# A third head of the down product in the norms' bank, a shorter series, and an earlier place for a layer's small parameters

## The chip, the cores and the metric

The kernel runs on one core of a Trainium2 chip, as one program. The core has a matrix engine (TensorE, in the views PE, with PEld for its weight loads), three engines for elementwise work (VectorE or DVE, ScalarE or ACT, GpSimd or POOL) and SyncE (SP), whose queue issues the DMA transfers here. Each engine works through its own queue of instructions in order; semaphores tie the queues together. The metric is the device time of one execution in microseconds; lower is better. The "span" is the time between the first and the last record of a profiled execution.

## What is computed

Two layers of a hybrid decoder run for one inference step, on a prompt of 512 tokens and on eight sequences of eight tokens that share the weights; all is fp32. Each layer is a feed-forward block, a mixer (sliding-window attention beside a gated linear recurrence) and a second feed-forward block, each ahead of it normed and modulated by vectors from a small conditioning product. Cut to what matters here:

```python
def swiglu(h, w_gate, w_up, w_down):
    return (jax.nn.silu(h @ w_gate) * (h @ w_up)) @ w_down
...
    x = x + FFN_RES * g1 * swiglu(modulate(x, sh1, sc1), w1_gate, w1_up, w1_down)
    h = modulate(x, sh2, sc2)
    z = h @ w_in
...
    xc, new_conv = causal_conv(xr, conv_buf, conv_w, conv_b)
    hs, h_last = rg_lru(xc, h0, w_rg, b_rg, w_ig, b_ig, lru_lambda)
...
    x = x + g2 * (merged @ w_out)
    x = x + FFN_RES * g3 * swiglu(modulate(x, sh3, sc3), w2_gate, w2_up, w2_down)
```

The model is 1024 wide, its hidden layer 2816. In the recurrence, `softplus(-lru_lambda)` is needed for 512 channels and two layers; it depends on parameters alone:

```python
    log_a = -RG_C * r.astype(jnp.float32) * jax.nn.softplus(-lam.astype(jnp.float32))
```

## The kernel before

**Products.** Activations are stored transposed: 128 features a tile, 576 tokens (64 of the eight sequences, then the prompt) in two halves, h=0 and h=1, of 288. An fp32 matrix product is made of three faster ones: each operand is split into a rounded high part, which ScalarE writes (L219), and the low rest, which VectorE or GpSimd subtracts (L220); then high by high, high by low and low by high are summed in one bank of PSUM, the matmul's accumulator memory. So a matmul needs splits of its weights (tiles `wh`, `wl`) and of its activations (tiles in the rings `t`, `u` or `hn`).

**Feed-forward block.** The hidden layer goes by pairs of 128 columns, eleven pairs to a block. A pair loads its gate and up weights (`load_pair`, L617). After the first one or two pairs of a block, which are made plainly, each of the two products of a pair is made by `quad` with seven block products instead of eight. That takes sums of weight blocks, on GpSimd (L849, tiles `P`), and sums of activation blocks, which `sums` prepares once a block on VectorE (L763): for each k of four, a sum `a` in bank tp, from it a sum `b` in bank nrm, from it a sum `c` in bank pv (in the very first block they stand in SBUF instead). The generator is drained by the first pair that wants the sums. In a quad, two of the block results accumulate in banks `pa` and `pe` (both of the name mm), two in banks of the name sc; ScalarE (L870, L882) and VectorE (L858 to L862) combine them, and the product of gate and up is split again into the two hidden halves (L220).

**Groups and heads.** Pairs are gathered into groups of four hidden tiles (two pairs) or of two (one pair): `GROUPS` is (4, 4, 4, 2, 4, 4) for the first block of the first layer and (2, 4, 4, 4, 4, 4) for the other three blocks. Behind a group come its down products: for each of eight output tiles m and each half h the product of the group's hidden tiles with the down weights, and `update` (L593, L595, L598, VectorE) adds the result to the residual stream, which empties the bank. So that TensorE has work while the group's last pair is still being combined, `head()` starts four of these products with the hidden tiles of the earlier pair (`slice(0, nf - 2)`), and `down` ends them later. Where a group has two hidden tiles, that slice is empty, so that the heads there only take their banks. `halves` is true for the last group of a block, and for a first group of width two: there the down products run all m of h=0 first, and then all m of h=1. In the last group of a block which has a norm behind it (three of four), TensorE's order is pinned, and the last quad's last product (`end_pair`) stands ahead of the third head.

**Banks.** There are eight banks of PSUM: three of the name mm, two sc, and one each of tp, pv and nrm. A tile of a name waits until the earlier tile in that bank has been read. The bank nrm serves the norms, the sums `b`, and one product of the first pair.

**Order.** A planner orders each engine's queue when the program is built, by estimated costs and by the order in which the Python code issues the work; pinned instructions keep a given order.

**Parameters of the recurrence.** `params()` fills one tile by a memset (L407) and fourteen small DMAs on SP's queue (L410 to L418), transposes it, and computes the softplus on tiles of 128x8: an exponential on ScalarE (L430, with a load of its function table) and then, on VectorE, a series for the logarithm (L433 to L440), whose result is kept for both layers. `layer_loads` (L946) clears a tile and issues six more DMAs. Both are called by `start`, in the first block of each layer, ahead of the pair of number START (L634); `params()` in the first layer alone.

Of the kernel before, what the change touches and what calls it, by code (L numbers as in the profile page):

```python
# [15 lines left out]
ALU = mybir.AluOpType  # L16
# [14 lines left out]
FT = DFF // P  # L31
GROUPS = ((4, 4, 4, 2, 4, 4), (2, 4, 4, 4, 4, 4))
NA = (1, 4)
START = 8
ADA0 = 3
PLAIN = ((2, 1), (1, 1))
LATE = (0, 0)
# [116 lines left out]
class Net:  # L154
# [249 lines left out]
    def params(self):  # L404
        nc, I = self.nc, self.I
# [20 lines left out]
        def c8(name):  # L426
            return self.const(name, [P, LC, DEPTH])
        y, s, s2, acc, mx = c8("sy"), c8("ss"), c8("ss2"), c8("sacc"), c8("smx")
# [4 lines left out]
        nc.vector.tensor_tensor(s, s, y, ALU.mult)  # L433
        nc.vector.tensor_tensor(s2, s, s, ALU.mult)
        n = 9
        nc.vector.tensor_scalar(acc, s2, 1.0 / (2 * n + 1), 1.0 / (2 * n - 1), ALU.mult, ALU.add)
        for i in range(n - 2, -1, -1):
            nc.vector.tensor_tensor(acc, acc, s2, ALU.mult)
            nc.vector.tensor_scalar(acc, acc, 1.0 / (2 * i + 1), None, ALU.add)
        nc.vector.scalar_tensor_tensor(acc, acc, 2.0, s, ALU.mult, ALU.mult)  # L440
        nc.vector.tensor_scalar(mx, lam, -1.0, 0.0, ALU.mult, ALU.max)
        self.sp2, self.spm4 = c8("sp2"), c8("spm4")
        nc.vector.tensor_tensor(acc, acc, mx, ALU.add)
# [177 lines left out]
    def ffn(self, l, ws, wd, s0, hn, pend, nxt, groups, ada_n, wo=None, open_next=None, start=None, raws=None, after=None):  # L621

        nc, I = self.nc, self.I
# [4 lines left out]
        for gi, nf in enumerate(groups):  # L628
            hid = []
            for fp in range(nf // 2):  # L630
                hts = [(self.slot([P, NT], F32R), self.slot([P, NT], F32R, "u")) for _ in range(2)]
                hid += hts
                pn = f0 // 2 + fp
                if start and pn == START:  # L634
                    start()
# [65 lines left out]
            box, heads = None, []  # L701
            pin = last and nxt is not None
            halves = last or gi == 0 and nf == 2

            def head():

                for n, (m, h) in enumerate(((0, 0), (1, 0), (2, 0), (3, 0)) if halves else ((0, 1), (1, 1), (0, 0), (1, 0))):
                    if n == 2 and (pin or not halves):
                        self.end_pair()
                    heads.append(self.ps(("mm", "sc")[len(heads) % 2]))  # L710
                    self.down_part(heads[-1], h, units[m], hid, nf, slice(0, nf - 2), pin)
                self.end_pair()

# [4 lines left out]
            for c0 in range(0, D, 2 * nw):  # L718
                raw = self.t("raw", [P, 2048]).rearrange("p (k c) -> p k c", k=nf)
                nc.sync.dma_start(raw, I[wd][l].rearrange("(f p) c -> p f c", p=P)[:, f0:f0 + nf, c0:c0 + 2 * nw])  # L720
                for c in range(0, 2 * nw, nw):
                    u = self.wsplit(raw[:, :, c:c + nw], (nf, nw), wo and not gi)
                    units += [(u[0][:, :, j * P:(j + 1) * P], u[1][:, :, j * P:(j + 1) * P]) for j in range(nw // P)]
                    if c0 + c == (HEAD * nw if halves else 0):
                        head()
                        if last:
                            self.hold = self.parts
                    if not halves:
                        for h in (1, 0):
                            for m in range((c0 + c) // P, len(units)):  # L730
                                down(m, h, ("mm", "sc")[m % 2])
# [808 lines left out]
```

## Time and profile before

| | us |
|---|---|
| median of three runs | 2165.23 (2163.7 to 2166.9) |
| the profiled execution | 2164.47 |
| its span | 2162.6 |
| TensorE busy in it | 2091.9 |
| VectorE busy | 1552.9 |
| ScalarE busy | 1022.0 |
| GpSimd busy | 774.9 |

A row of the page's groups, or of the timeline, names an engine, a line of the kernel, an operation, and tiles as out<-in. In the timeline the first number is the start in microseconds and the second the duration; a bracket at the end is the idle time of the engine just before, and what ended it. In the windows, after the stretch's bounds and length, each engine has its busy time and its number of instructions, and behind them stand the granted clock of TensorE (1.00 is full speed), the busy share of the DMA engines and the GB/s. Adjacent matmuls overlap in the records, so that the distance between starts, not the duration, is the price of one.

### The profile page before, as it was taken

The page shows a single profiled execution, that of the slowest core. Times are in us where ns is not written, and L with a number is a line of the kernel's source. Part 1 is how long each engine was busy: PE and PEld are TensorE (multiplying, and loading weights), DVE is VectorE, ACT ScalarE, POOL GpSimd, SP SyncE. Part 2 cuts the span into 40 slices and gives each one's busy share as a digit, 9 for nine tenths or more (in the row PEclk, how much of TensorE's full clock was granted, in tenths as well). Part 3 has the DMA queues.
Part 4 walks back from the last instruction along what each step waited for, and adds up shares of the span by engine and source line. Part 5 has one row for each costly group of instructions (what it writes and reads, how often), then busy time and mean ns, then how long its engine had stood idle before and what let it go on. Part 6 is the DMA issues. An engine that isn't in the chain of part 4 may idle for free.

```text
span 2162.6 us, 40524 instructions
## 1 busy us (share of the span) xinstructions
PE 2091.9 (97%) x15856; PEld 1976.5 (91%) x15856; DVE 1552.9 (72%) x3779; ACT 1022.0 (47%) x2348; POOL 774.9 (36%) x671
## 2 busy tenths in 40 slices
PE   6999999999999999999999999999999999999999
PEld 6889899999878988989999999999997899999998
DVE  5666767675787876576678966776667789677765
ACT  4333435356576433343354543444567664344432
POOL 2242323234426433233245342232552474323430
PEclk8999999999999999999999999999999999999999
DMA  9745633231212165463342323232312022223221
GB/s 306 267 146 182 219 116 130 78 118 46 69 53 80 66 247 195 174 217 137 118 147 69 110 66 98 79 117 79 98 43 79 22 79 79 99 79 117 81 76 45
DMA packets 162365, 250.11 MB, mean 116 GB/s; under 512 B 7276, under 2 KB 125436, under 8 KB 154975
## 3 DMA queue, kind: packets, MB, share of 16 engines
q1 hardware_dynamic: 162018, 247.46, 34.1%
q8 instruction: 124, 2.03, 0.4%
q14 instruction: 67, 0.54, 0.1%
q10 hardware_dynamic: 156, 0.07, 0.0%
HBM read 244.62 MB, written 4.87 MB: 115 GB/s over the span
## 4 chain that ended last, share of the span: by engine, by line
PE 84%; DVE 9%; ACT 3%; DMA 1%; issue 1%; POOL 1%; SPq 0%; ACTq 0%; DVEq 0%; POOLq 0%
PE ps_mm L843 25%; PE ps_mm L206 13%; PE ps_sc L933 11%; PE ps_mm L933 11%; PE ps_sc L843 10%; PE ps_sc L206 7%; DVE wl L220 3%; PE ps_pv L491 2%; PE ps_pv L206 2%; DMA raw<-in_w_ada_dram 1%; PE ps_nrm L206 1%; PE ps_tp L209 1%; ACT wh L219 1%; DVE u L220 1%; ACT t L219 1%
## 5 line engine op out<-in xcount | busy, mean ns | idle before, releaser
L849 POOL TENSOR_TENSOR P<-raw 128x512 f32<-128x512 f32 x156 | 229.2, 1482 | 714.3 <-DVE wl L220 383.1
L219 ACT CAST wh<-raw 128x512 fp32r<-128x512 f32 x498 | 296.7, 620 | 293.8 <-PE ps_sc L933 125.8
L220 DVE TENSOR_TENSOR wl<-raw,wh 128x512 fp32r<-128x512 f32 x408 | 336.5, 839 | 43.6 <-ACT wh L219 28.8
L219 ACT CAST wh<-P 128x512 fp32r<-128x512 f32 x312 | 187.2, 620 | 283.4 <-PE ps_sc L933 193.2
L220 DVE TENSOR_TENSOR wl<-P,wh 128x512 fp32r<-128x512 f32 x312 | 245.4, 803 | 63.4 <-ACT wh L219 56.1
L843 PE MATMUL ps_mm<-hn,wh 128*128 128x288 f32 x1248 | 256.0, 296 | 2.3 <-ACT wh L219 0.8
L843 PE MATMUL ps_sc<-hn,wh 128*128 128x288 f32 x1248 | 255.0, 296 | 0.0
L843 PE MATMUL ps_mm<-t,wh 128*128 128x288 f32 x936 | 221.9, 298 | 2.4 <-DVE ps_mm L861 1.7
L843 PE MATMUL ps_mm<-u,wh 128*128 128x288 f32 x936 | 220.8, 297 | 0.0
L843 PEld LDWEIGHTS ps_mm<-hn,wh 128*128 128x128 f32 x1248 | 199.8, 188 | 14.8 <-ACT t L870 2.9
L843 PEld LDWEIGHTS ps_sc<-hn,wh 128*128 128x128 f32 x1248 | 199.8, 188 | 9.6 <-issue 9.2
L933 PE MATMUL ps_sc<-t,wh 128*128 128x288 f32 x608 | 180.1, 296 | 5.7 <-DVE u L220 4.6
L843 PE MATMUL ps_mm<-u,wl 128*128 128x288 f32 x624 | 184.1, 295 | 0.0
L843 PE MATMUL ps_sc<-hn,wl 128*128 128x288 f32 x624 | 184.1, 295 | 0.0
L843 PE MATMUL ps_mm<-hn,wl 128*128 128x288 f32 x624 | 183.9, 295 | 0.0
L933 PE MATMUL ps_mm<-t,wh 128*128 128x288 f32 x608 | 180.6, 297 | 2.3 <-DVE u L220 1.8
L933 PE MATMUL ps_mm<-t,wl 128*128 128x288 f32 x608 | 179.6, 295 | 1.3 <-DVE wl L220 1.3
L933 PE MATMUL ps_mm<-u,wh 128*128 128x288 f32 x608 | 179.8, 296 | 0.2
L933 PE MATMUL ps_sc<-u,wh 128*128 128x288 f32 x608 | 179.3, 295 | 0.0
L933 PE MATMUL ps_sc<-t,wl 128*128 128x288 f32 x608 | 179.2, 295 | 0.0
L843 PEld LDWEIGHTS ps_mm<-t,wh 128*128 128x128 f32 x936 | 159.1, 189 | 12.1 <-issue 4.6
L849 POOL TENSOR_TENSOR P<-P,raw 128x512 f32<-128x512 f32 x78 | 114.4, 1466 | 154.4 <-DVE wl L220 152.1
(413 smaller groups left out, 5453.2 us busy)
## 6 DMA issues: line engine op xcount, KB each, us to landing
raw<-in_w_ada_dram SPq DMA_DIRECT2D x60, 1024.0 KB
raw<-in_w_gate_dram SPq DMA_DIRECT2D x44, 1024.0 KB
raw<-in_w_up_dram SPq DMA_DIRECT2D x44, 1024.0 KB
raw<-in_w_down_dram SPq DMA_DIRECT2D x44, 1024.0 KB
raw<-in_w_in_dram SPq DMA_DIRECT2D x14, 1024.0 KB
raw<-in_w_ada_dram SPq DMA_DIRECT2D x16, 512.0 KB
raw<-in_w_out_dram SPq DMA_DIRECT2D x4, 1024.0 KB
raw<-in_w_out_dram SPq DMA_DIRECT2D x8, 512.0 KB
```

The lines of the kernel that those rows point to most:

```text
L206: return self.pin(self.nc.tensor.matmul(*a, **k))
L209: return self.pin(self.nc.tensor.transpose(*a, **k))
L219: a = self.nc.scalar.copy(hi, src)
L220: b = (self.nc.gpsimd if pool else self.nc.vector).tensor_tensor(lo, src, hi.bitcast(F32), ALU.subtract)
L491: nc.tensor.matmul(acc[32 * j:32 * j + 32, :n], self.cT[:, k, :], raw[:, j * n:(j + 1) * n], start=(k == 0), stop=(k == KT - 1), tile_posi ...
L843: nc.tensor.matmul(ps[:, :HALF], a[x][:, k, :], b[k][y], start=start and k + n == 0, stop=k == 3 and n == 2, skip_group_check=True)
L849: nc.gpsimd.tensor_tensor(t, s[x] if x == 1 else x, s[y] if y == 2 else y, op)
L933: mm(ps[:, :HALF], u[x][:, f, :], hid[f][y][:, hs], start=f + n == 0, stop=f == nf - 1 and n == 2)
```

## The change

Three things change.

- The third of the four heads takes its bank by the name nrm instead of mm, wherever `halves` is true: in the last group of all four blocks, and in the first group of the three blocks that begin with a group of two.
- The logarithm's series is written with one fused instruction a coefficient, (acc + constant) * s2, in place of a product and an addition: one tensor_scalar, nine scalar_tensor_tensor and one more tensor_scalar for the factor of two, eleven instructions in place of eighteen.
- START goes from 8 to 6: the parameters and the layer's small loads are issued two pairs sooner, in both layers.

```diff
-START = 8
+START = 6
...
-        nc.vector.tensor_scalar(acc, s2, 1.0 / (2 * n + 1), 1.0 / (2 * n - 1), ALU.mult, ALU.add)
-        for i in range(n - 2, -1, -1):
-            nc.vector.tensor_tensor(acc, acc, s2, ALU.mult)
-            nc.vector.tensor_scalar(acc, acc, 1.0 / (2 * i + 1), None, ALU.add)
-        nc.vector.scalar_tensor_tensor(acc, acc, 2.0, s, ALU.mult, ALU.mult)
+        nc.vector.tensor_scalar(acc, s2, 1.0 / (2 * n + 1), None, ALU.mult)
+        for i in range(n - 1, 0, -1):
+            nc.vector.scalar_tensor_tensor(acc, acc, 1.0 / (2 * i + 1), s2, ALU.add, ALU.mult)
+        nc.vector.scalar_tensor_tensor(acc, acc, 1.0, s, ALU.add, ALU.mult)
+        nc.vector.tensor_scalar(acc, acc, 2.0, None, ALU.mult)
...
-                    heads.append(self.ps(("mm", "sc")[len(heads) % 2]))
+                    heads.append(self.ps(("mm", "sc", "nrm" if halves else "mm", "sc")[len(heads)]))
                     self.down_part(heads[-1], h, units[m], hid, nf, slice(0, nf - 2), pin)
```

## The prediction, made before the change was run

> **What bounds the kernel now.** I read the page's first lines, then the chain that ended last, then PE's rows among the waits, and last the stretches around the three places that the diff touches.
>
> ```profile
> span 2162.6 us, 40524 instructions
> PE 2091.9 (97%) x15856; PEld 1976.5 (91%) x15856; DVE 1552.9 (72%) x3779; ACT 1022.0 (47%) x2348; POOL 774.9 (36%) x671
> ...
> PE 84%; DVE 9%; ACT 3%; DMA 1%; issue 1%; POOL 1%; SPq 0%; ACTq 0%; DVEq 0%; POOLq 0%
> ```
> ```profile
> PE ps_mm L206 <- DVE u L220: 6.8, 3, 2.3
> PE ps_sc L933 <- DVE u L220: 4.6, 6, 3.5
> ```
> ```profile
> 270.00:280.00 10.00, 10.00 (x78) 10.00 (x77) 7.20 (x20) 2.29 (x4) 2.31 (x2) 1.00 0.15 50
> 280.00:290.00 10.00, 10.00 (x77) 10.00 (x77) 5.11 (x14) 1.18 (x3) 3.49 (x3) 1.00 0.01 2
> ```
> TensorE bounds it: 97% busy, 84% of the chain. The two waits (total us, times, longest) are nearly all that it loses to DVE's splits on the touched paths. The windows (columns: PE, PEld, DVE, ACT, POOL busy, granted clock, DMA share) give the price of one matmul in a full stretch: 10 us for 77 to 78, 0.13 us. So only a gap on PE, or a slowed PE, counts; everything else is cover. No edit changes the number of matmuls.
>
> **Edit 1, third head in nrm: the last groups.** PE's timeline (start, duration, ..., [idle before, releaser]) and DVE's and ACT's:
>
> ```profile
> 455.19 0.29 PE L843 MATMUL ps_mm<-u,wl 128*128 128x288 f32 x1
> 457.75 0.61 PE L206 MATMUL ps_mm<-t,wh 128*128 128x288 f32 x1 [2.27 <-DVE u L220]
> ...
> 1121.44 0.40 PE L206 MATMUL ps_mm<-t,wh 128*128 128x288 f32 x1 [2.27 <-DVE u L220]
> ...
> 1520.10 0.40 PE L206 MATMUL ps_mm<-t,wh 128*128 128x288 f32 x1 [2.26 <-DVE u L220]
> ```
> ```profile
> 457.24 0.82 DVE L220 TENSOR_TENSOR u<-ps_mm,t 128x288 fp32r<-128x288 f32 x2
> ```
> ```profile
> 452.35 0.40 ACT L882 COPY u<-ps_sc 128x288 f32<-128x288 f32 x1
> ```
> ```profile
> 455.00:461.00 6.00, 3.73 (x18) 3.50 (x17) 3.67 (x8) 2.32 (x5) 1.34 (x1) 0.72 0.06 11
> ```
> At the end of the three feed-forward blocks that have a norm after them, the third head finds all three mm banks held (pa and pe of the last quad, head one) until DVE's splits at 457.24 read them. Its hidden half and weights are ready, and the norms' bank is idle then. So the stalls go: 2.27 + 2.27 + 2.26 = 6.8. The first also trips the clock: 6.00 us at 0.72, 18 matmuls that need 18 x 0.13 = 2.34, so 6.00 - 2.34 - 2.27 = 1.4 lost beside the stall. Sum 8.2. The fourth head's sc bank is free since ACT's copy at 452.35. Late next are the remaining products, whose banks DVE empties; for that I keep back 0.7: **-7.5**. Bounds: -8.2, and -4 if half of each stall comes back one step later. The fourth block has no norm after it; nothing is taken there.
>
> **Edit 1 again: the first groups.** `halves` also holds for a first group of width two, which three of four blocks have. There the heads run no product; they only take banks, so the third one takes nrm for the whole product (2, 0). Behind it, in the order of the program, stand the activation sums (L763): per k three subtractions in tp, two in nrm, two in pv, each followed by a split. Before, nothing stood between them and nrm. That a bank's name is handed out in the order of the program shows elsewhere:
>
> ```profile
> 749.65 0.46 DVE L220 TENSOR_TENSOR t<-ps_pv,t 128x288 fp32r<-128x288 f32 x1 [0.31 <-ACT t L219]
> ```
> ```profile
> 750.89 1.92 PE L491 MATMUL ps_pv<-raw,cT 128*32 128x512 f32 x16
> ```
> The modulation's product starts in pv only behind the last sum's split in pv. In the second layer's first block the product (2, 0) is drained at 1180.16, while the sums have begun long before:
>
> ```profile
> 1168.01 0.45 DVE L763 TENSOR_TENSOR ps_nrm<-hn,ps_tp 128x288 f32<-128x288 f32 x1
> ...
> 1180.16 0.44 DVE L598 SCALAR_TENSOR_TENSOR xT<-ps_mm,mod,xT 128x224 f32<-128x224 f32 x1
> ...
> 1194.19 0.44 DVE L220 TENSOR_TENSOR t<-ps_pv,t 128x288 fp32r<-128x288 f32 x1
> 1194.56 0.44 DVE L220 TENSOR_TENSOR u<-ps_tp,u 128x288 fp32r<-128x288 f32 x1
> ```
> ```profile
> 1164.00:1181.00 17.00, 7.22 (x17) 9.39 (x12) 1.00 0.18 60
> 1181.00:1201.00 20.00, 4.70 (x11) 0.00 (x0) 1.00 0.09 25
> ...
> 715.00:730.00 15.00, 7.23 (x17) 8.88 (x11) 1.00 0.16 54
> ...
> 1775.00:1791.00 16.00, 7.23 (x17) 9.32 (x11) 1.00 0.18 60
> ```
> The windows (L763's instructions on DVE, then POOL) show 17 of 28 sums ahead of that point, in all three blocks. After the change only the first k's three and their split can stand there: the next k's tp tile waits for the nrm sum that reads the tp bank. So 14 subtractions and 5 splits move behind 1180.5. Back to back such instructions start 0.37 us apart (1194.19, 1194.56): 19 x 0.37 = 7.0 us. DVE there:
>
> ```profile
> 1178.00:1190.00 12.00, 12.00 (x90) 12.00 (x91) 10.57 (x37) 1.93 (x5) 1.86 (x3) 1.00 0.26 87
> 1190.00:1200.00 10.00, 10.00 (x74) 9.55 (x73) 9.69 (x22) 5.68 (x14) 4.29 (x4) 1.00 0.07 8
> 1200.00:1210.00 10.00, 9.54 (x68) 8.86 (x67) 10.00 (x13) 5.67 (x12) 6.37 (x5) 1.00 0.29 106
> ```
> 1.4 us are free until 1190 and 0.3 until 1200, none after. So the third k's splits, at 1194.19 the last, come some 5.4 us late, and with them the gate's copy on ACT and its product 6 on PE:
>
> ```profile
> 1194.74 0.39 ACT L870 COPY t<-ps_mm 128x288 f32<-128x288 f32 x1
> ```
> ```profile
> 1195.21 0.38 PE L843 MATMUL ps_mm<-u,wh 128*128 128x288 f32 x1
> ```
> PE can take little ahead of it (its next products want the same sums or weights that the same full DVE splits). 5.2 each, three blocks: **+15.5**. A wait that is queued on DVE also holds the updates and weight splits behind it. Bounds: 0, if DVE's splits of weights go into the hole at 1168 to 1180 in exchange; +25, if each stall brings the slowed clock too, by the first group's 1.4 and the 1.6 below, and the moved work is late by its whole 7.0: 3 x (7.0 + 1.4) = 25.
>
> **Edits 2 and 3, the series and its place.** START 6 puts the recurrence's parameters and the layer's small loads two pairs sooner. Now:
>
> ```profile
> 370.13 1.31 DVE L434 TENSOR_TENSOR ss<-ss 128x8 f32<-128x8 f32 x1
> ...
> 380.90 0.45 DVE L220 TENSOR_TENSOR u<-ps_sc,t 128x288 fp32r<-128x288 f32 x1
> ```
> ```profile
> 381.41 0.40 PE L933 MATMUL ps_sc<-t,wh 128*128 128x288 f32 x1 [3.47 <-DVE u L220]
> ```
> ```profile
> 381.00:386.00 5.00, 4.59 (x23) 4.59 (x24) 3.60 (x12) 1.83 (x5) 0.00 (x0) 0.66 0.59 198
> ```
> ```profile
> L438 DVE TENSOR_TENSOR sacc<-sacc,ss x8: 153/166/168, 372.7 to 379.9; 128x8 f32<-128x8 f32 x8
> L439 DVE TENSOR_SCALAR sacc<-sacc x8: 160/172/1157, 372.9 to 380.1; 128x8 f32<-128x8 f32 x8
> ...
> L440 DVE SCALAR_TENSOR_TENSOR sacc<-sacc,ss x1: 159/159/159, 380.8 to 380.8; 128x8 f32<-128x8 f32 x1
> ```
> The split at 380.90, behind the chain on DVE, costs PE 3.47 us, and then a low clock: 5.00 us hold 23 matmuls, 23 x 0.13 = 3.0, and 0.41 of the idle; 1.6 more. The series shrinks from 18 instructions to 11; the fused form took 159 ns, no more than either it replaces, so seven at 0.17, 1.2 us, go. That alone does not undo 3.47; the move does. In the new place, 260 to 290, DVE is busy 7.20 and 5.11 in the quoted windows: 7.7 us of slack for 11 instructions and some ten more, 21 x 0.17 = 3.6. SP's queue gets the memset's wait, 14 parameter loads and the layer's loads:
>
> ```profile
> 260.44 8.84 SPq L489 DMA_DIRECT2D raw<-in_w_ada_dram  x2
> 292.20 0.33 SPq L489 DMA_DIRECT2D raw<-in_w_ada_dram  x1
> ...
> 357.15 0.26 SPq L410 DMA_DIRECT2D t<-in_conv_b_dram  x1
> ...
> 361.32 0.25 SPq L418 DMA_DIRECT2D t<-in_k_gain_dram  x1
> ```
> They took 361.57 - 357.15 = 4.4 us for 14; SP has 292.20 - 269.28 = 22.9 free there. They cost nothing unless that memset waits past 288. POOL's memset (0.5 us) and ACT's two table loads lie beside PE's ten full microseconds. The second layer has no series of its own, and its loads move within the same slack. I take 3.47 + 1.6 = 5.1 less 0.6 for the handover: **-4.5**, bounds -5.1 and 0 (an equal stall in the new place).
>
> The row at 370.13 and the longest of L439, 1157 ns, show tiny instructions stretched seven times while POOL added operands. The Trainium skill, "SBUF — State Buffer", section "Who interferes with whom", speaks against the rewrite: an instruction with two SBUF inputs on VectorE, as all the new series' are, shuts out GpSimd and is shut out by it for whole instructions. The trace agrees for the two-input product (1.31), and shows the stretch on one-input steps too (1.16). By the rule the series could pay 1.16 at every POOL instruction; by the windows POOL runs 5.8 us in five of them there, under the 7.7 of slack, and the sum stays.
>
> The low clock follows the gaps of 3.47 and, at 457.75, of 2.27; at 1121.44 and 1520.10 the same gap left it. "TensorE: Matmul & The Clock Gate", Part 1, of the Trainium skill asks for no idle beyond some 3 us in a free-running window of 3.4 us. The 3.47 agrees, the 2.27 does not; by the rule alone the term of 1.4 would be missing from edit 1.
>
> **Sum.** -7.5 + 15.5 - 4.5 = +3.5 on the profiled execution's 2164.47 (span 2162.6 and 1.9 around it): 2168.0. The median shown is 0.76 higher, so 2168.8: **2169**.
>
> **Rivals.** (1) The sums' wait is covered: PE is full at 1178 to 1200, DVE puts weight splits into the hole, and the first groups cost under 4. For it: PE does not stall before 1200 now. Against: DVE is full from 1190. Then 2165.2 - 12 + 0 to 4 = 2153 to 2157: **faster**. (2) The sums are late by the whole 7.0 and the clock falls behind each stall, a first-group term of 20 to 25: 2165.2 - 12 + 20 to 25 = 2173 to 2178, and 2181 where edit 1 earns only its -4 besides, **slower**; it decides when a gap passes about 2 us, as at 457.75. (3) The change does not do what it says: the third head gets its bank, but the fourth head or the remainder waits for the same DVE splits, or the parameters stall PE by 3.47 in the new place. Only half of edit 1 or none of edits 2 and 3 remains: +3.5 to 4.5 more, about 2173.
>
> **How the numbers follow.** Forecast 0.50, rival one 0.25, rival two 0.13, rival three 0.12. A measurement tells about 0.2%, 4.3 us, so the same is 2160.9 to 2169.6. The forecast's own range, 2163 to 2176, puts 0.27 of its 0.50 there, 0.20 above, 0.03 below; rival one 0.21 below, 0.04 in it; two and three above, 0.25 but for 0.01. Faster 0.25, same 0.31, slower 0.44. The range runs from within rival one to the end of rival two, 2155 to 2181.
>
> **What would show it.** Edit 1: no gap behind the last product that ends each of the three blocks (before 457.75, 1121.44 and 1520.10 here), and no low clock behind the first. First groups: L763 in nrm starting behind the update of (2, 0), few of its instructions ahead, and PE gaps before gate's products of the next pair; if PE has none there, rival one holds. Edits 2 and 3: the series at 260 to 295, no gap at 381. I would be wrong above all if the sums do not wait for nrm, or if a hidden queue puts nrm's third head elsewhere than in those groups.

## The result: 13.4 us faster, and the profile after

| | before | after |
|---|---|---|
| median, us | 2165.24 (6 runs) | 2151.80 (6 runs, 2151.32 to 2155.68) |
| ratio, with its 95% interval | | 0.9941 [0.9930, 0.9952] |
| the profiled execution | 2164.47 | 2151.38 |
| its span | 2162.6 | 2149.6 |

The forecast was 2169, with a range of 2155 to 2181: the measured 2151.80 lies below it. The page of the changed kernel, its first lines and the chain that ended last, and of its waits the one that is left of the two quoted before:

```profile
span 2149.6 us, 40505 instructions
PE 2088.8 (97%) x15856; PEld 1974.2 (92%) x15856; DVE 1552.8 (72%) x3772; ACT 1021.7 (48%) x2348; POOL 773.4 (36%) x671
...
PE 86%; DVE 8%; ACT 3%; issue 1%; POOL 1%; DMA 1%; SPq 0%; ACTq 0%; DVEq 0%
```
```profile
PE ps_sc L933 <- DVE u L220: 0.9, 4, 0.2
```

All engines do the same work as before, to 0.2%; TensorE just idles less. The wait for the third head (6.8 us in three gaps) is gone from the list, and the wait of the down products behind the parameters fell from 4.6, with a longest of 3.5, to 0.9.

Where the time went is read from equal marks: both kernels have 448 updates of the residual stream (the last instruction of `update`, L598, behind the down products and the mixers' output products), and the start of the n-th in one is set beside that of the n-th in the other.

| mark | before | after | after minus before |
|---|---|---|---|
| first update | 105.50 | 107.20 | +1.70 |
| ahead of the old place of the parameters | 320.53 | 322.75 | +2.22 |
| behind it | 388.17 | 384.62 | -3.55 |
| ahead of the first block's last group | 405.09 | 401.48 | -3.61 |
| behind it | 479.00 | 471.65 | -7.35 |
| around the second block's first group | 669.31, 801.45 | 661.93, 794.75 | -7.38, -6.70 |
| around its last group | 1063.58, 1141.33 | 1055.82, 1131.14 | -7.76, -10.19 |
| around the third block's first group | 1141.33, 1240.50 | 1131.14, 1230.28 | -10.19, -10.22 |
| around its last group | 1467.35, 1540.01 | 1457.04, 1527.34 | -10.31, -12.67 |
| around the fourth block's first group | 1730.20, 1851.19 | 1717.62, 1838.19 | -12.58, -13.00 |
| in the fourth block's last group | 2151.20 | 2138.15 | -13.05 |

So the parameters' place gave -3.55 - 2.22 = -5.8. Of that, 0.3 is no gain: TensorE's four transposes of the parameters (L422, 366.91 to 367.17 in the kernel before) now stand at 291.33, ahead of the mark at 322.75. The three last groups gave -3.7, -2.4 and -2.4, together -8.5, and the three first groups +0.7, 0.0 and -0.4, together +0.2. The +1.7 at the first mark is not the change's: up to 266 us every engine has the same instructions in the same order in both kernels. In their windows near the start (before, then after) TensorE's clock stays low for longer in this execution.

```profile
34.00:39.00 5.00, 5.00 (x88) 4.60 (x87) 1.12 (x5) 0.00 (x0) 0.00 (x0) 0.98 1.09 348
```
```profile
34.00:39.00 5.00, 5.00 (x76) 4.30 (x75) 0.29 (x1) 0.00 (x0) 0.00 (x0) 0.66 1.09 348
```

The timeline of TensorE at the end of the first block, with the windows of 6 us there and of 5 us at the old place of the parameters (PE, PEld, DVE, ACT, POOL busy, granted clock, DMA share, GB/s):

```profile
451.59 0.30 PE L843 MATMUL ps_mm<-u,wl 128*128 128x288 f32 x1
451.73 0.29 PE L206 MATMUL ps_nrm<-t,wh 128*128 128x288 f32 x1
...
452.51 0.30 PE L206 MATMUL ps_sc<-t,wh 128*128 128x288 f32 x1
...
453.31 0.29 PE L206 MATMUL ps_mm<-t,wh 128*128 128x288 f32 x1
```
```profile
450.00:456.00 6.00, 6.00 (x48) 6.00 (x47) 3.92 (x11) 2.32 (x5) 0.39 (x1) 1.00 0.01 3
```
```profile
381.00:386.00 5.00, 5.00 (x40) 5.00 (x40) 4.18 (x10) 1.94 (x4) 0.00 (x0) 1.00 0.09 16
```

The third head follows the last product 0.14 us later, in nrm; the fourth head and the remaining products follow without a gap. The window held 18 matmuls at a clock of 0.72 before and holds 48 at 1.00 now; the other one 23 at 0.66 before, and 40 now.

Now the point that the forecast turned on. VectorE's rows that empty the bank nrm by an `update` (L593 is its first instruction) are these four in the whole trace, and the windows of the sums (L763, on DVE and then POOL) are the ones quoted before, shifted by the lead:

```profile
456.36 0.22 DVE L593 TENSOR_TENSOR ps_nrm<-ps_nrm,mod 128x64 f32<-128x64 f32 x1
...
1115.78 0.22 DVE L593 TENSOR_TENSOR ps_nrm<-ps_nrm,mod 128x64 f32<-128x64 f32 x1
...
1512.00 0.22 DVE L593 TENSOR_TENSOR ps_nrm<-ps_nrm,mod 128x64 f32<-128x64 f32 x1
...
2121.48 0.22 DVE L593 TENSOR_TENSOR ps_nrm<-ps_nrm,mod 128x64 f32<-128x64 f32 x1
```
```profile
1153.80:1170.80 17.00, 7.23 (x17) 9.36 (x12) 1.00 0.18 58
...
707.30:722.30 15.00, 7.89 (x17) 8.21 (x11) 1.00 0.15 54
...
1762.50:1778.50 16.00, 7.24 (x17) 9.32 (x11) 1.00 0.19 55
```

Four, all in last groups; none in a first group. And 17 sums stand where 17 stood. The first groups never took the bank. The code says why, in the line that calls `head()`: `if c0 + c == (HEAD * nw if halves else 0)`. HEAD is 2; a group of two hidden tiles has nw = 1024 // 2 = 512, so the heads would start at column HEAD * nw = 1024, and c0 + c takes only 0 and 512. In a group of four, nw is 256 and column 512 is reached. `halves` is true in the first groups, but `head()` isn't called there. So "wherever `halves` is true", in the list of changes above, is too wide: the new bank is taken in the last groups alone.

The series in its new place, by tile (count, duration min/median/max in ns, first and last start):

```profile
L438 DVE SCALAR_TENSOR_TENSOR sacc<-sacc,ss x8: 158/166/166, 297.4 to 298.8; 128x8 f32<-128x8 f32 x8
...
L439 DVE SCALAR_TENSOR_TENSOR sacc<-sacc,ss x1: 167/167/167, 299.0 to 299.0; 128x8 f32<-128x8 f32 x1
```

No instruction is stretched there: GpSimd has none between 289.8 and 310.3. The forecast had the series at 260 to 295; it stands a little later, at 297 to 299.

### The profile page after: what moved, and what is told of

It is laid out like the page before. It is cut to its first block, busy times and chain, and to the rows that moved or that the text cites. A ratio compares the mean times of both kernels' runs of the same rounds, so it can differ in the third digit from the quotient of the medians.

```text
span 2149.6 us, 40505 instructions
## 1 busy us (share of the span) xinstructions
PE 2088.8 (97%) x15856; PEld 1974.2 (92%) x15856; DVE 1552.8 (72%) x3772; ACT 1021.7 (48%) x2348; POOL 773.4 (36%) x671
## 4 chain that ended last, share of the span: by engine, by line
PE 86%; DVE 8%; ACT 3%; issue 1%; POOL 1%; DMA 1%; SPq 0%; ACTq 0%; DVEq 0%
PE ps_mm L843 27%; PE ps_mm L206 13%; PE ps_sc L933 11%; PE ps_mm L933 10%; PE ps_sc L843 10%; PE ps_sc L206 7%; DVE wl L220 3%; PE ps_pv L491 2%; PE ps_pv L206 2%; PE ps_nrm L206 1%; PE ps_tp L209 1%; ACT wh L219 1%; DMA raw<-in_w_ada_dram 1%; DVE u L220 1%; DVE t L1421 0%
## 5 line engine op out<-in xcount | busy, mean ns | idle before, releaser
L219 ACT CAST wh<-raw 128x512 fp32r<-128x512 f32 x498 | 296.7, 620 | 289.8 <-PE ps_sc L933 129.8
L220 DVE TENSOR_TENSOR wl<-raw,wh 128x512 fp32r<-128x512 f32 x408 | 341.5, 851 | 41.4 <-ACT wh L219 26.8
```

The source lines that it names most:

```text
L219: a = self.nc.scalar.copy(hi, src)
L220: b = (self.nc.gpsimd if pool else self.nc.vector).tensor_tensor(lo, src, hi.bitcast(F32), ALU.subtract)
```

## The experiments

The theory after the result: the term of the first groups did not exist, and the other two stand about as forecast. The rival: the sums do wait for nrm somewhere, but the wait is covered. Each time is a median, and each gain is against runs of the kernel before that were made beside it on the same chip.

### The bank alone

```diff
-                    heads.append(self.ps(("mm", "sc")[len(heads) % 2]))
+                    heads.append(self.ps(("mm", "sc", "nrm" if halves else "mm", "sc")[len(heads)]))
```

> The kernel before with the third head's bank alone changed. Theory: the first groups of width two never start heads, so the edit acts in the last groups only, and is worth what the traces of the two kernels differ by there: about -3.7, -2.5 and -2.4 at the three pinned blocks, -8.6 together: 2156 to 2157 against 2165; the sums keep their place, and the gap of 3.5 at 381 stays. Rival (the sums wait for nrm, but the cost is hidden): the same time, but with fewer of the sums ahead of the first group's updates. Rival (the gain of the change hangs together): under 5 us of gain.

Measured: 2159.10 against 2165.50, ratio 0.9970 [0.9958, 0.9981]: -6.4, less than the 8 to 9 that were expected. By the marks, the three last groups gave -3.7, -2.2 and -2.3 in its trace, -8.3 together; the gap of 3.47 at the parameters stays. The trace loses time in two other places: 2.7 us ahead of the mark at 320.53, where it has the same instructions in the same order as the kernel before, and 2.9 in the second mixer, to which the last experiment returns. The sums' rival falls: in this trace too an `update` empties nrm only in the four last groups.

### The series and its place, with the old banks

```diff
-START = 8
+START = 6
...
+            nc.vector.scalar_tensor_tensor(acc, acc, 1.0 / (2 * i + 1), s2, ALU.add, ALU.mult)
```

(The whole hunk of the series is as in the change.)

> The kernel before with the shorter series and START 6, and the heads' banks as before. Theory: the parameters' gap goes with its slow clock, -5.7 at 381, less about 0.9 that the new place costs near 270 to 320: -4.9, so 2160 to 2161; the three gaps of 2.27 stay. Rival (the gain of the change hangs together): a different number, so that this and the bank alone do not add up to -13.4.

Measured: 2158.67, ratio 0.9971 [0.9960, 0.9982]: -6.8, somewhat more than the 4.9 that were expected, and with the bank alone -13.2, against -13.4 for both. The two add up. The marks give -5.7 for the parameters' place. The three gaps of 2.27 stay, but the slow clock behind them sits elsewhere. They end at 452.22, 1112.29 and 1512.37 in this kernel. Its windows there, in the order second, third, first:

```profile
1112.00:1118.00 6.00, 5.71 (x31) 5.71 (x32) 3.37 (x10) 2.63 (x6) 1.35 (x1) 0.72 0.47 156
1512.00:1518.00 6.00, 5.63 (x31) 5.64 (x32) 3.31 (x10) 2.27 (x6) 1.35 (x1) 0.72 0.48 141
452.00:458.00 6.00, 5.78 (x43) 5.78 (x44) 4.79 (x16) 3.81 (x10) 2.54 (x2) 1.00 0.48 148
```

In the profile of before, the gap at 457.75 tripped the clock and the ones at 1121.44 and 1520.10 did not; here it is the reverse, with the same gaps. So the 1.4 that the forecast gave to the first of them belongs to no gap in particular: each of them may draw it.

### Heads in the first groups, with nrm and with mm

What the prediction took the change to do, made real: the heads are started in the first groups as well.

```diff
-                    if c0 + c == (HEAD * nw if halves else 0):
+                    if c0 + c == (HEAD * nw if last else nw if halves else 0):
```

> The changed kernel, with the heads also started in the first groups of width two, the third one in nrm: what the prediction took the change to do. Theory (the forecast's mechanism is right, only its place did not exist): 14 sums and 5 splits move behind the update of (2, 0) in three blocks, some 5 us each: +15, so 2160 to 2172. Rival (a bank taken early costs nothing there, since VectorE puts weight splits into the hole): within 3 us of the next kernel, which has the same heads in mm.

The control has the same line, and takes the third head's bank there by the name mm, as before:

```diff
-                    heads.append(self.ps(("mm", "sc", "nrm" if halves else "mm", "sc")[len(heads)]))
+                    heads.append(self.ps(("mm", "sc", "nrm" if last else "mm", "sc")[len(heads)]))
```

> The changed kernel, with the heads also started in the first groups of width two, the third one in mm there and in nrm in the last groups. Control for the kernel with nrm: both theories expect the changed kernel's time within 2 us, 2150 to 2154, as the heads of a group of two run no product and only take the banks sooner.

Measured: with nrm 2181.67, ratio 1.0075 [1.0062, 1.0087], 16.2 slower than before; with mm 2154.24, ratio 0.9947 [0.9934, 0.9961]. In the control every engine has the same instructions in the same order as in the changed kernel, so its 2.4 us above 2151.80, just outside the 2 that were expected, are scatter. The bank in those three groups costs 27.4 us. So the mechanism of the forecast is real, and dearer than the 15.5 that it was given, or the 2160 to 2172 expected here; the marks say 8.8, 11.3 and 10.5 in the three groups, and 0.3, 0.6 and 0.1 in the control. VectorE in the third block of the kernel with nrm (timeline, then the windows of the sums):

```profile
1164.48 0.46 DVE L763 TENSOR_TENSOR ps_tp<-ps_tp,hn 128x288 f32<-128x288 f32 x1
...
1177.07 0.45 DVE L598 SCALAR_TENSOR_TENSOR xT<-ps_nrm,mod,xT 128x224 f32<-128x224 f32 x1
...
1183.10 0.45 DVE L763 TENSOR_TENSOR ps_nrm<-hn,ps_tp 128x288 f32<-128x288 f32 x1
```
```profile
1160.00:1177.00 17.00, 1.39 (x3) 5.78 (x7) 1.00 0.07 19
1177.00:1200.00 23.00, 8.46 (x21) 5.14 (x5) 0.95 0.23 79
```

Three sums stand ahead of the update that empties nrm, as the forecast had it, where 17 stood; so it is in all three groups. The next sum in nrm starts 6 us behind that update, among the last updates. Who is late behind them is not who the forecast named. GpSimd, TensorE, and TensorE's windows:

```profile
1189.23 0.80 POOL L220 TENSOR_TENSOR hn<-acc,hn 128x288 fp32r<-128x288 f32 x1 [18.29 <-ACT hn L219]
```
```profile
1196.15 0.40 PE L843 MATMUL ps_mm<-hn,wh 128*128 128x288 f32 x1 [1.96 <-ACT hn L219]
1197.16 0.40 PE L843 MATMUL ps_mm<-hn,wh 128*128 128x288 f32 x1 [0.61 <-POOL hn L220]
1199.64 0.61 PE L843 MATMUL ps_mm<-hn,wh 128*128 128x288 f32 x1 [1.95 <-ACT hn L219]
...
1202.95 0.61 PE L843 MATMUL ps_mm<-u,wh 128*128 128x288 f32 x1 [1.58 <-ACT wh L219]
```
```profile
1195.00:1210.00 15.00, 9.44 (x43) 8.32 (x44) 11.09 (x27) 6.72 (x17) 7.34 (x8) 0.66 0.21 71
```

GpSimd's own sums, at the end of `sums`, overwrite in place the activation block b12 (the first four feature tiles of h=1). VectorE's sums in tp read b12, so the overwriting waits for them, k by k: GpSimd is idle for 18.29 us until ScalarE has cast the high part, at 1188.72, right behind VectorE's last reading of it (1188.17, 0.46 long). The product that reads the new b12 is number 7, which stands ahead of number 6, the one that the forecast named. The gaps are 1.96 + 0.61 + 1.95 + 1.58 = 6.1, the first 0.8 of it ahead of the window; a small one of 0.27 at 1200.52 joins them, and then comes the clock. In the window's 15 us TensorE is busy for 9.44 and idle for 5.6; its 43 matmuls need 43 x 0.13 = 5.6 at full speed, so that 9.4 are lost there, 5.6 to gaps and 3.8 to the low clock. The two other groups have the same four gaps, to some 0.3 us each, and a clock of 0.68 around them (738 to 754 and 1814 to 1830).

### The series and the move apart

The series alone, in its old place (its hunk alone):

> The kernel before with the shorter series alone, in its old place. Theory: seven instructions of 0.17 us leave VectorE's queue and the ones beside GpSimd's operand sums stay stretched, so the gap at 381 shrinks from 3.47 by about 1.2 and its slow clock may stay: -1.2 to -2.8, 2162.5 to 2164. Rival (the shared port: an instruction with two SBUF inputs pays a GpSimd instruction each): more of the nine fused instructions are stretched past 1 us than the five of before, and the gap stays or grows: 2165 or more.

Measured: 2163.99 against 2166.55, ratio 0.9986 [0.9977, 0.9995]: -2.6. By tile, and the gap on TensorE:

```profile
L438 DVE SCALAR_TENSOR_TENSOR sacc<-sacc,ss x8: 166/168/1212, 371.6 to 376.0; 128x8 f32<-128x8 f32 x8
L436 DVE TENSOR_SCALAR sacc<-ss x1: 1312/1312/1312, 370.2 to 370.2; 128x8 f32<-128x8 f32 x1
```
```profile
380.81 0.61 PE L933 MATMUL ps_sc<-t,wh 128*128 128x288 f32 x1 [3.01 <-DVE u L220]
```

The fused instructions are stretched to the same 1.2 us, but no more of them: the eight take 4.59 us together, which is three of 1.2 and five of 0.17. With L436 that makes four, as many as the operand sums that GpSimd runs in that stretch, and as many as were stretched in the kernel before (L434, L436 and two of L439). So in these two traces the number of GpSimd's instructions sets the price, not the number or the form of the small ones, and the rival (nine stretched) falls. The gap shrinks by 0.46 only, against 1.2 expected: the seven instructions that left stood partly between weight splits, where one delays the next by 0.07 (in the kernel before, a coefficient at 377.01 and the next split at 377.08), not by its 0.17; 7 x 0.07 = 0.5. By the marks this trace has -0.7 at the parameters, -1.4 at the first of the three gaps of 2.27, where it drew no slow clock, and +1.5 at the third, where it did. So the median fell into the expected range by luck: the trace gives the series 0.7, and the rest of the 2.6 (interval 1.1 to 5.0) is not shown to be the series'. The runs' mean granted clock was 0.993, against 0.992 in the ones beside them.

The move alone, with the long series:

```diff
-START = 8
+START = 6
```

> The kernel before with START 6 alone, the long series in the new place. Theory: the move does nearly all of what the two edits did together (2158.7), since VectorE has slack in the new place: within 1.5 us of that, 2158 to 2160.5. Rival (the series matters in the new place too): 2162 or more, with a gap on TensorE near 271 or 317 that is over 1 us longer than in the changed kernel.

Measured: 2159.29, ratio 0.9965 [0.9952, 0.9978]: -7.3 alone, where series and move together gave -6.8. The gap at 381 is gone, and the marks give -5.8 at the old place, as in the changed kernel. The move does it all.

The changed kernel with the long series back:

> The changed kernel with the long series back: bank in nrm and START 6. Theory (the series is worth nothing once it is moved): the changed kernel's 2151.8 within 1.5. Rival: slower by 3 or more.

Measured: 2153.38, 1.6 above the changed kernel's median where 1.5 was allowed; but the ratio is 0.9930 [0.9917, 0.9943], and the changed kernel's 0.9941 lies inside that interval. Once it is moved, the shorter series is worth nothing that these runs can tell.

The changed kernel with START 4:

```diff
-START = 6
+START = 4
```

> The changed kernel with START 4. Theory: in the new place of START 6 the parameters cost about 0.9, seen as longer gaps near 271 and 317; a place still earlier only moves such a cost: within 2 of 2151.8. Rival (any place with more slack is better): faster than 2150.

Measured: 2152.14, ratio 0.9932 [0.9919, 0.9945]; the same, and not under the rival's 2150. The series then runs at 214 to 218, and the gap near 315 stays, at 1.42 (1.52 in the changed kernel, 1.06 in the kernel before). It is not the series' cost: in the next experiment, with the same instructions in the same order as the changed kernel, it is 0.33.

### The last groups alone, and what a repetition scatters

```diff
-                    heads.append(self.ps(("mm", "sc", "nrm" if halves else "mm", "sc")[len(heads)]))
+                    heads.append(self.ps(("mm", "sc", "nrm" if last else "mm", "sc")[len(heads)]))
```

> The changed kernel with nrm asked for in the last group alone (if last, in place of if halves). Theory (heads are never started in a first group of width two, so that part of the condition does nothing): the changed kernel's 2151.8 within 2, and the same places of the sums. Rival (the first groups still pay something in the changed kernel): faster than 2149.

Measured: 2154.83 against 2166.27, ratio 0.9942 [0.9929, 0.9956], where the change had 0.9941. As heads are not started in the first groups, this is the changed kernel again: every engine has the same instructions in the same order. Its median is still 3.0 us higher, outside the 2 that were expected (the kernel before was 1.0 higher beside it), and its profiled span 5.6. By the marks nearly all of the 5.6 arises in the two mixers: 2.9 between 471.65 and 618.04, 2.6 between 1527.34 and 1673.97. The window over the second mixer of this kernel, and then of the changed kernel:

```profile
1610.00:1640.00 30.00, 27.13 (x197) 23.65 (x197) 20.72 (x78) 14.56 (x41) 10.35 (x10) 0.83 0.28 71
```
```profile
1610.00:1640.00 30.00, 27.13 (x215) 23.93 (x213) 21.50 (x85) 16.15 (x48) 8.47 (x7) 0.94 0.27 71
```

The same stretch held a granted clock of 0.83 in one execution and 0.94 in the other. Such stretches scatter all the medians here.

They may also take back a part of what the bank earns. In all eleven traces TensorE has a gap of 2.2 us at the same place of the second mixer. Over the 12 us that start with the end of this gap, the clock is 1.00 in the four traces with the old banks; in the seven with nrm it is 0.57 four times, 0.86 twice and 1.00 once. The kernel before, and then the bank alone:

```profile
1629.00:1641.00 12.00, 11.32 (x95) 10.47 (x96) 8.52 (x41) 6.46 (x17) 5.08 (x4) 1.00 0.32 103
```
```profile
1623.00:1635.00 12.00, 11.23 (x62) 9.74 (x63) 5.22 (x27) 5.34 (x14) 3.87 (x4) 0.57 0.25 89
```

The medians point the same way. The three pairs of kernels that differ by the bank alone give -6.4, -6.6 (the changed kernel against the series and its place) and -5.9 (the changed kernel with the long series against the move alone), where the marks at the last groups give -8.3 and -8.5. Whether the bank makes the mixer's gap lower the clock more often, or these traces fell so by chance, no run here shows.

## Why the prediction was wrong

**The step that failed** stands at the head of the part on the first groups: "There the heads run no product; they only take banks, so the third one takes nrm for the whole product (2, 0)." The heads are not started there at all. `halves` and the empty slice were read, the condition on HEAD at the call was not, and a term of +15.5 was built on it. Without it, the working's own other terms are -7.5 - 4.5 = -12.0 on 2164.47, 2152.5 for the profiled execution, where 2151.38 was measured. That this is so close is partly luck: both terms came out larger at their places, and the slow start of that execution (+1.7), which is not the change's, took most of the surplus back. The prediction had named the outcome as its foremost way of being wrong ("if the sums do not wait for nrm"), but not this reason.

**The first groups' mechanism** was right, where it is made to apply: three sums ahead of the update, as worked out, and a bank's name handed out in the order of the program. Its size was not: 27.4 instead of 15.5, above the bound of 25. Its own steps missed that GpSimd's overwriting of b12 hangs on the same sums, so that product 7 stalls ahead of product 6; and the forecast itself left out the low clock, which follows in each of the three groups and which only the bound had. The bound at the other end, VectorE doing weight splits in the hole instead, did not hold.

**Edit 1 in the last groups**: forecast -7.5, marks -8.5 and -8.3 in two traces, a little beyond the bound of -8.2; by the medians -5.9 to -6.6, with the difference perhaps in the mixers' clock, which the forecast did not consider. The 0.7 kept back for banks that VectorE empties late was not lost. That the slow clock belongs to the first gap was chance; over the runs each of the three gaps may have it.

**Edits 2 and 3**: forecast -4.5, marks -5.8 at the old place, beyond the bound of -5.1. Against it stand 0.5 that are lost between the marks at 269 and 320: 0.3 for the four transposes that moved there, and a longer gap near 317, which the same program did not have in another trace. So -5.3 to -5.5 remain, about the gap of 3.47 and its slow clock; the 0.6 taken off for the handover did not show. The move was given nearly all of it, and has all of it. The seven instructions at 0.17 were overvalued: 0.46 of gap, not 1.2.

**The port.** The prediction said that all of the new series' instructions have two inputs; nine of the eleven have. By the Trainium skill ("SBUF — State Buffer", "Who interferes with whom") GpSimd can hold up a VectorE instruction with two SBUF inputs for a whole instruction, and a tensor_scalar, which has one, in a mode that takes both read ports as well. These rows agree: four GpSimd instructions, four stretched ones on VectorE, and among them one with a single input (L436, 1312 ns), though no trace shows in which mode it ran. So the fused form adds nothing to the price.

**The rivals.** The time fell below that of rival one (2153 to 2157), but its reason is wrong: there was no wait to cover. And where the wait was made, it was not covered. Rivals two and three did not occur: the clock stayed at 1.00 behind the last group, the fourth head followed at once, and the series stalled nothing.

## What to carry to other kernels

A condition in a diff says where an edit may act; whether the line is reached there depends on every condition on the way to it, with its numbers put in (here 2 x 512 against a column that stops at 512). Ahead of pricing the dearest term of a change, follow the call down to it. And a long-lived bank that is shared under a name should be given only to work that ends before the next user of that name stands in the order of the program: the third head in nrm is worth 6 us by the medians (8.5 by the marks) at the ends of three blocks, and costs 27 at their beginnings.

## What the hardware showed that was not expected

- A gap of 2.27 us on TensorE lowers its clock in some executions and not in others: at one of three gaps in the kernel before, and at the two other ones in the kernel with the old banks, for 1.4 to 1.5 us each. Two other kernels had it at the third gap, and at the first and third. The same program had 0.83 and 0.94 over the same 30 us of a mixer, and spans 5.6 us apart.
- While GpSimd runs an operand sum of 1.3 us, a VectorE instruction on 128x8 that takes 0.17 us alone takes 1.15 to 1.31, one instruction for each of GpSimd's.
- A small instruction between large ones on VectorE delays the next by 0.07 us (377.01 to 377.08 in the kernel before), where in a chain of its own kind one follows the other after 0.20 us (375.71 to 375.92).
